# A DRAM-to-SBUF load that writes four copies of a triangular system to the partitions: one transfer, or one for each quarter

## The chip, the cores and the metric

The kernel runs on one core of one Trainium2 chip. The metric is device time in microseconds (us) of one execution, lower is better. The kernel before takes 2083.18 us, the median of three runs (2080.98 to 2087.81). The inputs lie in DRAM when the time starts, and the outputs must lie in DRAM when it ends.

## The reference

One layer of a hybrid encoder is applied to 2048 prompt frames and 32 sample frames of width 1024. The layer normalises its input, projects it to 6160 columns, runs two mixers on the result, attention over a band of nine 64-frame chunks (branch A) and a gated delta rule (branch B), and merges their outputs. The change touches branch B alone, and there the inverse of a unit lower triangular matrix for each head and each block of 64 frames:

```
m = jnp.einsum('nbhid,nbhjd->nbhij', k_beta, kb) * decay * strict
eye = jnp.eye(blk, dtype=f32)
t_inv = lax.linalg.triangular_solve(eye + m, jnp.broadcast_to(eye, m.shape),
                                    left_side=True, lower=True, unit_diagonal=True)
u = jnp.einsum('nbhij,nbhjd->nbhid', t_inv, v_beta)
```

The state of the rule then goes through the blocks in order, one step for each 64 frames.

## The kernel before

The prompt is done in two halves of 1024 frames; the sample frames ride with the second. Each half has a stage for branch B (`phase_b`) and one for branch A (`phase_a`). The large projections run beside both, so that TensorE (PE) always has matmuls to do: weights are loaded (`wraw`), scaled and split into two fp16 parts by ScalarE (ACT) and GpSimd (POOL), and multiplied into the PSUM banks `pj`. A last stage merges the branches and writes the output.

Python generators describe the pieces of work. A planner (`Flow`) runs them against a model of the engines and the transfers, and the order in which it emits instructions is the order of each engine's queue: every engine works through its queue in order and waits where an operand isn't there yet. All the transfers that this document speaks of are issued by SyncE's queue (SP in the profile, SPq for its issuing instructions), line 283, in `dma`. A transfer signals that it has landed on one of eight completion lanes, used in turn (`DMAHW0` to `DMAHW7`); an instruction that needs its data waits on that lane, and SP waits, before it gives a lane to a new transfer, until the lane's last transfer has landed.

In `phase_b` a block is one pair of heads and 512 frames, that is 16 triangular systems of 64 x 64. There are eight blocks in each half, and one more for the sample frames: 17 in all. For each block:

- `system` computes the matrices (`p_c`, on 128 partitions) and stores their diagonal 32 x 32 sub-blocks to DRAM, `sol_p`: 32 rows, one for each sub-block, of 1024 numbers each. Four transfers.
- `solve` clears `sys_u` on POOL, loads `sol_p` into `sys_p` four times over, to partitions 0 to 31, 32 to 63, 64 to 95 and 96 to 127 (lines 1236 and 1237), so that partition 32g + s holds system s and works on its columns g, g + 4, g + 8 and so on, and calls `substitute`.
- `substitute` is the forward substitution: 31 steps on VectorE (DVE) of a multiply into `sys_t` and a subtract from `sys_u`. The first instruction that reads `sys_p` is the 128 x 31 multiply `sys_t<-sys_p,sys_u`.
- The result goes to DRAM (`sol_u`), comes back in another shape (`tu`), and `inverse` builds the 64 x 64 inverses `u_bd` with it.
- `chain` runs the recurrence over the blocks. Each step is a ping-pong between PE and DVE: matmul into bank `x`, `r` on DVE, matmul with `u_bd`, `vn` on DVE, matmul, `state` on DVE. `tail` then normalises the outputs, loads the gate (`gb<-z`) and stores the product (`g<-gb`).

All of this shares DVE's queue with the convolutions (`acc`), the evacuations of projections (`zb`) and the weights' scales (`w_scale`).

Of the kernel before, what the change touches and what calls it, by code (L numbers as in the profile page):

```python
# [268 lines left out]
def trunk(ctx: ExitStack, tc: tile.TileContext, x_p, x_s, cache_k, cache_v, st_conv, st_gdn,  # L269
# [11 lines left out]
    def dma(dst, src, eng=nc.sync):  # L281

        eng.dma_start(dst, src)  # L283
        size = 2 if dst.dtype == F16 else 4
        n = size
        for k in dst.shape:
            n *= k

        n = max(n, n // (size * dst.shape[-1]) * 768)
        return flow.transfer("SP" if eng is nc.sync else "S", n)  # L290
# [495 lines left out]
    def phase_b(half):  # L786
# [438 lines left out]
        def solve():  # L1225
            while True:
                k, t = yield from q_sys.get()
                sys_p = bp.tile([P, 32, 32], F32, tag="sys_p", bufs=2, name="sys_p")
                sys_u = bp.tile([P, 8, 32], F32, tag="sys_u", bufs=2, name="sys_u")
                sys_t = bp.tile([P, 8, 32], F32, tag="sys_t", bufs=2, name="sys_t")  # L1230
                G.memset(sys_u[:], 0.0)
                for g in range(4):
                    G.memset(sys_u[g * 32:(g + 1) * 32].rearrange("p r i -> p (r i)")[:, g::36], 1.0)
                yield t
                p0 = pd[k.n % (2 * NP)][:]
                yield dma(sys_p[:].rearrange("p j i -> p (j i)"),
                          bass.AP(p0.tensor, p0.offset, [[0, 4], [1024, 32], [1, 1024]]))
                yield from substitute(sys_p, sys_u, sys_t)
                for g in range(4):
                    t = dma(ud[k.n % (2 * NP)][:].rearrange("s (r g i) -> g s r i", g=4, i=32)[g], sys_u[g * 32:(g + 1) * 32])  # L1240
                flow.start(inverse(k, t))

        def substitute(sys_p, sys_u, sys_t):
            for j in range(31):
                nr = j // 4 + 1
                w = 31 - j
                if nr == 1:
                    V.tensor_scalar(out=sys_t[:, 0, 0:w], in0=sys_p[:, j, j + 1:32], scalar1=sys_u[:, 0, j:j + 1],
                                    scalar2=None, op0=ALU.mult)
                else:  # L1250
                    V.tensor_tensor(out=sys_t[:, 0:nr, 0:w], in0=sys_u[:, 0:nr, j:j + 1].to_broadcast([P, nr, w]),
                                    in1=sys_p[:, j:j + 1, j + 1:32].to_broadcast([P, nr, w]), op=ALU.mult)
                yield
                V.tensor_tensor(out=sys_u[:, 0:nr, j + 1:32], in0=sys_u[:, 0:nr, j + 1:32],
                                in1=sys_t[:, 0:nr, 0:w], op=ALU.subtract)
                yield
# [179 lines left out]
        for g in (worker(todo), worker(decays), prep(), local(), solve(), solve()):  # L1436
            flow.start(g)
# [878 lines left out]
```

## Time and profile before

| | before |
|---|---|
| median of three runs | 2083.18 us |
| the profiled execution's own time | 2081.13 us |
| its span, first to last instruction | 2079.4 us |
| PE busy | 1969.9 us (95%) |
| DVE busy | 1456.5 us (70%) |
| ACT busy | 977.0 us (47%) |
| POOL busy | 709.3 us (34%) |
| mean granted clock of PE | 0.982 |
| DMA engines' mean share | 31.7% (the queue of SP's transfers) |
| loads `sys_p<-sol_p` | 17 of 512.0 KB, issued from 141.3 to 1247.5 us |

Times inside the execution count from its first instruction. An engine's waits are told as idle time before an instruction, with the one that released it in brackets. A stretch row gives busy time and count of instructions of each engine, the clock granted to PE (1.00 is full), the mean busy share of the core's 16 DMA engines and the bytes moved per second.

### The profile page before, as it was taken

The numbers are of one execution on the slowest core, as the hardware profiler recorded it, in microseconds if no ns is written. First come the engines' busy times: TensorE is split into PE (matmuls) and PEld (weight loads), VectorE is DVE, ScalarE is ACT, GpSimd is POOL, SyncE is SP. The second block draws the span as 40 slices with busy tenths as digits, with TensorE's granted clock in tenths as the row PEclk, the third lists the DMA queues.
The fourth block names the chain that finished last, engine by engine and source line by source line (L and its number), as shares of the span: only waits on it lengthen the run. The fifth ranks groups of instructions, "written<-read, shape, count | busy, mean of one in ns | idle before, by whom it ended". The sixth has DMA issues, their size and how long they took to land. (4 is left out here: it accounts for less than half of the span.)

```text
span 2079.4 us, 41810 instructions
## 1 busy us (share of the span) xinstructions
PE 1969.9 (95%) x15098; PEld 1419.4 (68%) x15098; DVE 1456.5 (70%) x4673; ACT 977.0 (47%) x2098; POOL 709.3 (34%) x1075
## 2 busy tenths in 40 slices
PE   4899999999999999899999899999999999999998
PEld 3455666667465666566677676767667678999996
DVE  7579888874267667768998887347657677655565
ACT  5565645444466668564544434346566642111110
POOL 5254443423322123334333323311110224644443
PEclk9899999999999999999999999999999999999999
DMA  3132332232323333222233233332332345433331
GB/s 109 62 98 80 98 107 65 82 82 87 121 68 122 92 87 101 66 72 73 78 85 88 73 91 95 97 91 76 87 89 82 108 139 196 135 105 113 111 123 48
DMA packets 197724, 196.53 MB, mean 95 GB/s; under 512 B 79623, under 2 KB 147571, under 8 KB 197517
## 3 DMA queue, kind: packets, MB, share of 16 engines
q1 hardware_dynamic: 197516, 193.85, 31.7%
q8 instruction: 119, 1.95, 0.4%
q14 instruction: 89, 0.72, 0.1%
HBM read 135.91 MB, written 50.53 MB: 90 GB/s over the span
## 5 line engine op out<-in xcount | busy, mean ns | idle before, releaser
L260 PE MATMUL pj<-hi,whi 128*128 128x512 f16 (+2 forms) x1992 | 654.3, 344 | 12.6 <-POOL whi L260 2.4
L260 PE MATMUL pj<-hi,wlo 128*128 128x512 f16 (+2 forms) x1952 | 644.4, 342 | 2.0 <-POOL wlo L260 1.9
L260 PEld LDWEIGHTS <-whi 128*128 128x128 f16 x3984 | 412.7, 105 | 222.2 <-issue 11.1
L260 PE MATMUL pj<-lo,whi 128*128 128x512 f16 (+2 forms) x1992 | 461.3, 339 | 0.0
L260 POOL TENSOR_TENSOR wlo<-wraw,whi 128x256 f16<-128x256 f32 x384 | 263.8, 708 | 570.9 <-ACT whi L260 328.4
L260 PEld LDWEIGHTS <-wlo 128*128 128x128 f16 x1952 | 207.1, 106 | 112.6 <-issue 11.2
L260 ACT CAST mh<-sg 128x256 fp32r<-128x256 f32 x64 | 26.0, 407 | 273.7 <-DVE sg L260 273.7
L260 ACT ACTIVATE wraw<-wraw,w_scale 128x1024 f32<-128x1024 f32 (+1 forms) x98 | 111.5, 1138 | 64.9 <-DVE w_scale L260 51.9
L260 ACT CAST ph<-b 128x512 f16<-128x512 f32 (+2 forms) x224 | 92.9, 422 | 100.2 <-PE b L260 95.4
L260 PE MATMUL a<-ghi,whi 128*128 128x256 f32 (+1 forms) x512 | 132.5, 290 | 4.9 <-DVE sg L260 4.7
L260 DVE TENSOR_TENSOR pl<-b,ph 128x512 f16<-128x512 f32 (+2 forms) x224 | 107.2, 485 | 37.9 <-ACT ph L260 36.8
L260 PE MATMUL a<-ghi,wlo 128*128 128x256 f32 (+1 forms) x512 | 130.6, 286 | 1.1 <-DVE wlo L260 1.1
L260 ACT CAST whi<-wraw 128x512 f16<-128x512 f32 (+1 forms) x196 | 119.6, 611 | 23.4 <-PE pj L260 20.5
L260 DVE TENSOR_TENSOR sys_u<-sys_u,sys_t 128x60 f32<-128x60 f32 (+24 forms) x527 | 123.3, 240 | 6.1
L260 POOL TENSOR_TENSOR w_scale<-w_scale,mhalf 128x1 f32<-128x1 f32 x49 | 32.4, 662 | 257.0 <-DVE w_scale L260 204.0
L260 ACT ACTIVATE sb<-sb,mx,unit 128x640 f32<-128x640 f32 (+4 forms) x128 | 108.8, 851 | 20.7 <-DVE mx L260 20.3
L260 DVE SCALAR_TENSOR_TENSOR acc<-raw,cwT,acc 128x512 f32<-128x512 f32 x144 | 112.0, 777 | 5.2 <-ACT acc L260 4.1
L260 DVE TENSOR_TENSOR sys_t<-sys_u,sys_p 128x60 f32<-128x60 f32 (+20 forms) x459 | 111.2, 246 | 5.9
L260 PEld LDWEIGHTS a<-ghi,whi 128*128 128x128 f32 x512 | 98.2, 192 | 7.3 <-DVE sg L260 7.0
L260 ACT COPY v_t<-o 128x64 f32<-128x64 f32 x132 | 27.6, 209 | 157.0 <-PE o L260 113.1
L260 PE MATMUL b<-ident,sb 128*128 128x128 f32 x560 | 99.3, 277 | 1.9 <-DVE ga L260 0.9
L260 PEld LDWEIGHTS a<-ghi,wlo 128*128 128x128 f32 x512 | 97.8, 191 | 1.9 <-DVE wlo L260 1.6
(350 smaller groups left out, 4237.0 us busy)
## 6 DMA issues: line engine op xcount, KB each, us to landing
wraw<-in_w_in SPq DMA_DIRECT2D x192, 256.0 KB
sg<-sig SPq DMA_DIRECT2D x112, 128.0 KB
sig<-sig SPq DMA_DIRECT2D x44, 256.0 KB
sys_p<-sol_p SPq DMA_DIRECT2D x17, 512.0 KB
x<-in_x_p SPq DMA_DIRECT2D x16, 512.0 KB
xt<-in_x_p SPq DMA_DIRECT2D x16, 512.0 KB
out_y_p<-xt SPq DMA_DIRECT2D x16, 512.0 KB
glo<-g SPq DMA_DIRECT2D x14, 512.0 KB
```

Source lines behind the costliest of these rows:

```text
L260: r = f(*a, **k)
```

## The change

The one transfer to 128 partitions, whose source pattern names the 32 rows four times (`[0, 4]`, `[1024, 32]`, `[1, 1024]`), becomes four transfers of the same 32 rows, each to one quarter of the partitions. The bytes written, 512 KB for a block, stay the same.

```
                 yield t
                 p0 = pd[k.n % (2 * NP)][:]
-                yield dma(sys_p[:].rearrange("p j i -> p (j i)"),
-                          bass.AP(p0.tensor, p0.offset, [[0, 4], [1024, 32], [1, 1024]]))
+
+                for g in range(4):
+                    t = dma(sys_p[g * 32:(g + 1) * 32].rearrange("p j i -> p (j i)"),
+                            bass.AP(p0.tensor, p0.offset, [[1024, 32], [1, 1024]]))
+                yield t
                 yield from substitute(sys_p, sys_u, sys_t)
```

The planner's order comes out the same: PE, DVE, ACT and POOL have the same instructions in the same order in both kernels, and SP has the same transfers in the same order, with three more at each of the 17 places. What moves is the lane that a transfer gets, and with it the names of the lanes that are waited for.

SP's queue at the eighth block (first half; `z` and `gb` belong to the tail and the gate, `wraw` to the next weights), before and then changed:

```order
L283 DMA z_87<-zb 128x512 [waits DVE_49]
L283 DMA sys_p<-sol_p_621 128x1x1024 [waits DMAHW6_49,DMAHW7_49,DMAHW5_49,DMAHW0_49]
L283 DMA wraw<-in_w_in 128x512 [waits DMAHW3_49,Activation_49,Pool_49]
L283 DMA wraw<-in_w_in 128x512 [waits DMAHW4_49]
L283 DMA gb<-z_86 64x2x256 x2
L283 DMA z_87<-zb 128x512 [waits DVE_49]
```

```order
L283 DMA z_87<-zb 128x512 [waits DVE_49]
L283 DMA sys_p<-sol_p_621 32x1024 [waits DMAHW4_49,DMAHW5_49,DMAHW3_49,DMAHW2_49]
L283 DMA sys_p<-sol_p_621 32x1024 [waits DMAHW0_49]
L283 DMA sys_p<-sol_p_621 32x1024 [waits DMAHW1_49]
L283 DMA sys_p<-sol_p_621 32x1024
L283 DMA wraw<-in_w_in 128x512 [waits Activation_49,Pool_49]
L283 DMA wraw<-in_w_in 128x512
L283 DMA gb<-z_86 64x2x256
L283 DMA gb<-z_86 64x2x256 [waits DMAHW6_49]
L283 DMA z_87<-zb 128x512 [waits DMAHW7_49,DVE_49]
```

The first quarter still waits for the four stores of `sol_p`; behind the quarters come the same transfers as before.

SP's queue at the seventh block of the second half, before and then changed:

```order
L283 DMA gcb<-gc_dram 64x512 [waits DMAHW5_49]
L283 DMA sys_p<-sol_p_10523 128x1x1024 [waits DMAHW6_49,DMAHW7_49,DMAHW1_49,DMAHW0_49]
L283 DMA gb<-z_85 64x2x256 x2
L283 DMA z_86<-zb 128x240 [waits DVE_49]
L283 DMA wraw<-in_w_in 128x512 [waits DMAHW2_49,Activation_49,Pool_49]
```

```order
L283 DMA gcb<-gc_dram 64x512 [waits DMAHW7_49]
L283 DMA sys_p<-sol_p_10547 32x1024 [waits DMAHW2_49,DMAHW3_49,DMAHW1_49,DMAHW0_49]
L283 DMA sys_p<-sol_p_10547 32x1024 x3
L283 DMA gb<-z_85 64x2x256 [waits DMAHW4_49]
L283 DMA gb<-z_85 64x2x256 [waits DMAHW5_49]
L283 DMA z_86<-zb 128x240 [waits DMAHW6_49,DVE_49]
L283 DMA wraw<-in_w_in 128x512 [waits DMAHW7_49,Activation_49,Pool_49]
```

The loads `gb<-z` now stand four transfers behind the first load of `sys_p` instead of one, and wait for lanes by name.

DVE's queue at that block, before and then changed (`state` is a step of the recurrence, which waits for PE):

```order
L260 SCALAR_TENSOR_TENSOR v_s<-e,acc 128x32 [waits Activation_49]
L260 TENSOR_SCALAR sys_t<-sys_p,sys_u 128x31 [waits DMAHW6_49]
L260 SCALAR_TENSOR_TENSOR state<-state,sc,x 128x64 [waits PE_49]
L260 TENSOR_TENSOR sys_u<-sys_u,sys_t 128x8x3 [waits DVE_49]
L260 TENSOR_TENSOR sys_u<-sys_u,sys_t 128x31 [waits DMAHW1_49,DMAHW7_49,DMAHW0_49,DVE_49]
```

```order
L260 SCALAR_TENSOR_TENSOR v_s<-e,acc 128x32 [waits Activation_49]
L260 TENSOR_SCALAR sys_t<-sys_p,sys_u 128x31 [waits DMAHW2_49,DMAHW3_49,DMAHW1_49,DMAHW0_49]
L260 SCALAR_TENSOR_TENSOR state<-state,sc,x 128x64 [waits PE_49]
L260 TENSOR_TENSOR sys_u<-sys_u,sys_t 128x8x3 [waits DVE_49]
L260 TENSOR_TENSOR sys_u<-sys_u,sys_t 128x31 [waits DVE_49]
```

The instructions stand where they stood; the first multiply waits for four lanes instead of one.

## The prediction

> **What bounds the kernel now.** I read the page first, then the waits, then three stretches of the queues.
>
> ```profile
> PE 1969.9 (95%) x15098; PEld 1419.4 (68%) x15098; DVE 1456.5 (70%) x4673; ACT 977.0 (47%) x2098; POOL 709.3 (34%) x1075
> sys_p<-sol_p SPq DMA_DIRECT2D x17, 512.0 KB
> ```
>
> PE sets the time: it is idle for 2079.4 - 1969.9 = 109.5 us in all, so a change off PE can only give back a part of that, plus what PE loses when its clock is lowered. The list of waits says what the 17 loads cost directly:
>
> ```profile
> DVE sys_t L260 <- DMA sys_p<-sol_p: 9.4, 3, 4.8
> ACT sig L260 <- DMA z<-zb: 4.8, 1, 4.8
> ```
>
> So 14 of the 17 loads land before DVE asks for them and are worth nothing there; three are late, by 9.4 us together. The second row matters because of where it lies, as the third place shows. The load itself, first block, in SP's queue and by stretches (columns: stretch, busy us and count for PE, PEld, DVE, ACT and POOL, PE's clock, DMA share, GB/s):
>
> ```profile
> 141.26 0.63 SPq L283 DMA_DIRECT2D sys_p<-sol_p  x1
> 152.53 0.81 SPq L283 DMA_DIRECT2D wraw<-in_w_in  x2
> ...
> 141.00:143.00 2.00, 2.00 (x14) 1.13 (x13) 1.52 (x5) 1.42 (x3) 0.13 (x1) 1.00 0.93 340
> 147.00:149.00 2.00, 2.00 (x11) 0.90 (x10) 1.83 (x6) 1.72 (x4) 1.94 (x5) 1.00 0.25 102
> 149.00:152.00 3.00, 3.00 (x15) 1.35 (x14) 3.00 (x7) 1.54 (x4) 2.03 (x3) 1.00 0.01 5
> ```
>
> Nothing was issued between 141.26 and 152.53, so what moves from 147 to 149 us is this load: a share of 0.25, 4 engines of 16, at 102 GB/s, while other transfers just before it reached 0.93 and 340 GB/s. Its 524,288 bytes need 5.1 us at the one rate and 1.5 us at the other. It keeps four engines busy while twelve are idle, and whatever is issued behind it also needs those four.
>
> The three late places. The last number of a DVE or PE row is the idle time before it.
>
> ```profile
> 424.99 0.56 SPq L283 DMA_DIRECT2D sys_p<-sol_p  x1
> 437.48 0.24 DVE L260 TENSOR_SCALAR sys_t<-sys_p,sys_u 128x31 f32<-128x31 f32 x1 [4.25 <-DMA sys_p<-sol_p]
> 437.72 0.28 DVE L260 SCALAR_TENSOR_TENSOR r<-x,negc,v_t 128x64 f32<-128x64 f32 x1
> 438.06 0.44 PE L260 MATMUL x<-r,u_bd 128*128 128x64 f32 x2 [3.43 <-DVE r L260]
> ...
> 1183.53 0.56 SPq L283 DMA_DIRECT2D sys_p<-sol_p  x1
> 1195.00 0.24 DVE L260 TENSOR_SCALAR sys_t<-sys_p,sys_u 128x31 f32<-128x31 f32 x1 [4.83 <-DMA sys_p<-sol_p]
> 1195.16 0.27 DVE L260 SCALAR_TENSOR_TENSOR state<-state,sc,x 128x64 f32<-128x64 f32 x1
> 1195.48 0.69 PE L260 MATMUL x<-state,k_bd 128*128 128x64 f32 x2 [4.48 <-DVE state L260]
> ...
> 975.33 0.56 SPq L283 DMA_DIRECT2D sys_p<-sol_p  x1
> 975.94 8.33 SPq L283 DMA_DIRECT2D z<-zb  x2
> 987.30 0.48 DVE L260 TENSOR_SCALAR sys_t<-sys_p,sys_u 128x31 f32<-128x31 f32 x1 [0.37 <-DMA sys_p<-sol_p]
> 987.63 0.69 ACT L260 ACTIVATE sig<-pj,w_half 128x512 f32<-128x512 f32 x1 [4.80 <-DMA z<-zb]
> 988.37 0.28 PE L260 MATMUL pj<-hi,whi 128*128 128x272 f16 x1 [0.90 <-ACT sig L260]
> ```
>
> Call them A (425), B (1183) and C (975). From issue to use the load takes 437.48 - 424.99 = 12.49, 1195.00 - 1183.53 = 11.47 and 987.30 - 975.33 = 11.97 us. At A and B the recurrence stands behind the late multiply in DVE's queue (`r`, `state`), and PE stands behind the recurrence with all its projections. At C a store of `z` issued 0.61 us behind the load lands just when the load does, and holds a buffer that ACT, and then PE, needs.
>
> PE's idle time isn't the whole price:
>
> ```profile
> 438.00:442.00 4.00, 3.94 (x18) 3.44 (x19) 2.39 (x17) 0.96 (x1) 0.56 (x1) 0.57 0.22 79
> 442.00:446.00 4.00, 3.82 (x23) 2.17 (x21) 3.12 (x14) 1.90 (x6) 2.30 (x4) 1.00 0.21 33
> 1195.50:1199.60 4.10, 4.10 (x19) 3.14 (x20) 2.43 (x15) 1.38 (x3) 0.00 (x0) 0.51 0.35 110
> 1199.60:1204.00 4.40, 4.40 (x47) 3.78 (x46) 2.83 (x15) 1.94 (x4) 0.00 (x0) 1.00 0.46 98
> ```
>
> After each of the two long stalls PE works for some 4 us at about half its clock, busy for 3.94 of 4.00 and 4.10 of 4.10 us, so this is lost too.
>
> **The change, part by part.** *What a load costs then.* No row of before shows a 32-row load to a quarter, so I bound it.
>
> ```profile
> 1.52 1.77 SPq L283 DMA_DIRECT2D x<-in_x_p  x4
> 5.28 0.69 DVE L260 BATCH_NORM_STATS2 st<-x 128x6 f32<-128x512 f32 x1 [0.46 <-DMA x<-in_x_p]
> 1703.74 2.60 DMA sg<-sig
> 1726.88 6.68 DMA xt<-in_x_p
> 441.05 2.54 SPq L283 DMA_DIRECT2D sol_u<-sys_u  x4
> sg<-sig SPq DMA_DIRECT2D x112, 128.0 KB
> xt<-in_x_p SPq DMA_DIRECT2D x16, 512.0 KB
> ```
>
> Four loads of rows of 4 KB are issued in 1.77 us, 0.44 each; four issues of many small pieces take 2.54 us, 0.64 each. So the last quarter goes out 1.3 to 1.9 us after the first. From there a load of a quarter's size, 128 KB, takes 2.60 us in the chain of waits (`sg`). A load of all 512 KB, the first `x`, was used 3.76 us after its issue (5.28 - 1.52), with three like it behind it; the longest in the chain took 6.68 (`xt`). The last quarter is there at 1.3 + 2.6 = 3.9 us at best and 1.9 + 6.68 = 8.6 at worst after the first issue. I take 5: the quarters are like `sg` in size and like `x` in company.
>
> *What that removes.* DVE is ready for the load 12.49 - 4.25 = 8.24 us after its issue at A, 11.47 - 4.83 = 6.64 at B, 11.97 - 0.37 = 11.60 at C. At 5 us all three waits go. At 8.6 us A keeps 0.4 and B 2.0 us. The lowered clock goes with the stalls.
>
> - A: 3.43 idle + 4.00 x (1 - 0.57) = 1.72, together 5.15 us.
> - B: 4.48 + 4.10 x (1 - 0.51) = 2.01, together 6.49 us.
> - C: 0.90 us; the store of `z` goes out about 1.3 us later, behind the quarters, and finds all the engines soon free.
>
> The Trainium skill, page TensorE: Matmul & The Clock Gate, section Part 1: The HAM clock gate, says that the clock is halved after an idle window of about 3.4 us that runs freely, whatever the kernel does. By that, a gap of 3.43 us as at A meets a whole window only by chance, and the sum would be 1.72 us smaller in executions where it doesn't; the profiled one has the halved clock at both places, and the sum goes by it.
>
> *What it adds.* 51 issues on SP, 51 x 0.44 = 22 us over the execution. SP has room for them (nothing goes out from 141.9 to 152.5), and only what stands directly behind a load is later, by 1.3 us; it lands earlier all the same, since it no longer sits behind 5 us of transfer on four engines. DVE's first multiply waits for four lanes, three waits more:
>
> ```profile
> L260 DVEq EVENT_SEMAPHORE  x3: 21/50/50, 437.5 to 437.7; - x3
> ```
>
> 51 x 0.05 = 2.6 us at most on DVE, mostly while it would wait anyway, and DVE is idle for 30% of the span. I put it at nothing; if it all fell on the path it would be 2.6 us.
>
> *What is late next.* PE's work after A and B must be able to start earlier. These are the stretches behind them:
>
> ```profile
> 442.00:540.00 98.00, 97.17 (x705) 63.54 (x704) 45.95 (x192) 41.80 (x88) 34.02 (x51) 1.00 0.32 93
> 540.00:860.00 320.00, 310.62 (x2412) 192.43 (x2411) 219.85 (x770) 203.03 (x429) 84.10 (x126) 0.99 0.31 92
> 1199.60:1290.00 90.40, 87.57 (x783) 66.58 (x782) 76.64 (x324) 36.20 (x86) 29.55 (x50) 1.00 0.34 90
> 1290.00:1600.00 310.00, 304.72 (x2755) 217.31 (x2754) 177.32 (x617) 169.91 (x397) 53.44 (x82) 1.00 0.29 83
> ```
>
> PE is busy for 97 to 99% there, so it, and no other engine, sets the pace, and DVE moves up with it. After B DVE is at 85% (76.64 of 90.40); if anything takes some of B back, it is DVE. Nothing in this kernel starts at a fixed time, so an earlier PE stays earlier.
>
> Sum: 5.15 + 6.49 + 0.90 = 12.5 us, from the profiled execution's own 2081.13 (span 2079.4) to 2068.6. That execution lies 2.05 us under the median of the three runs, 2083.18; against the median the forecast is 2070.6. With the bounds (A and B keep 2.4 us, the 2.6 us of lane waits) the loss is at most 5 us: 2075.6. On the other side nothing reaches beyond the sum but the spread of the runs.
>
> **The rivals.** *The gain is half.* The next wait takes what the load gives back: DVE after B, or a shorter gap of PE that still lowers its clock. For it speaks DVE at 85%, against it that PE has no gap in the rows after either place. Worth B or A alone, about 6 us: 2077.
>
> *The quarters queue behind one another.* If four transfers follow each other with the full 2.60 us each, the last one lands 4 x 2.60 = 10.4 us after the first issue; A keeps 10.4 - 8.24 = 2.2 and B 10.4 - 6.64 = 3.8 of their waits. Gain about 3 us: 2080, no change that can be told. Against it: the four `x` loads above went out in 1.77 us, and the first was there in 3.76. The Trainium skill, page DMA: Bandwidth & Descriptors, section Rules for kernel authors, speaks for this rival: two transfers to disjoint halves of the partitions serialize on the same 16 engines, and one transfer to 128 partitions is better. The same section says that an outermost dimension of size c below 16, such as a broadcast of c copies, keeps a transfer on c engines at most; the share of 0.25 agrees with that, and then the one transfer is not the 16-engine transfer that the first rule has in mind.
>
> *Slower: the quarters get no more engines.* If a quarter, too, runs on 4 of the 16 engines, and all on the same four, the bytes take the same 5.1 us and everything is 3 x 0.44 = 1.3 us later: three stalls grow by 1.3, and so do the stores and loads behind. Worth 3 x 1.3 = 4 us and more clock: 2087 or more. It decides from the point where the last quarter lands more than 11.5 us after the first issue. Against it: the source's outermost dimension of four copies is gone, and the rows' share of 0.93 comes from loads without it.
>
> **How the numbers follow.** A change under 0.3%, 6.2 us, can't be told from none here. Chances: the forecast 0.74 (2065 to 2076), half the gain 0.13, queueing quarters 0.08, no more engines 0.05. The range takes in the spread of the runs below the sum, 2064.5, and half the gain above, 2078. Faster by over 0.3% (under 2076.9): nearly all of the forecast and half of the half gain, 0.80; within 0.3%: the other half, the queueing quarters and a part of the rest, 0.16; slower 0.04.
>
> **What would show it.** Right: the first multiply of `sys_t` follows the last issue of `sys_p` by less than 7 us where DVE waits for it, or DVE has no such wait left; stretches after an issue have a DMA share far over 0.25; PE's gaps at A and B are gone and its clock is 1.00 behind them; SP has 68 issues of `sys_p` of 128 KB. Wrong: `sys_t<-sys_p` still stalls by more than 2 us at B; or both stalls are gone and PE has new gaps of like size within the next 100 us; or transfers behind `sys_p` land later than now.

## The result and the profile after

| | before | after |
|---|---|---|
| median of the runs compared | 2084.25 us | 2071.72 us |
| lowest and highest | 2080.98 to 2088.89 | 2068.95 to 2076.6 |
| the profiled execution's own time | 2081.13 us | 2071.35 us |
| its span | 2079.4 us | 2069.6 us |
| PE busy | 1969.9 us | 1969.5 us |
| span less PE's busy time | 109.5 us | 100.1 us |

The ratio of after to before is 0.9941, with a 95% interval of 0.9922 to 0.996: the changed kernel is faster by 8 to 16 us. The two medians differ by 12.53 us.

From the page of after (engines; DMA issues with their median from issue to landing), and from its view of the tile `sys_p` (shortest, median and longest time of a quarter from issue to landing):

```profile
PE 1969.5 (95%) x15098; PEld 1420.1 (69%) x15098; DVE 1458.4 (70%) x4673; ACT 978.4 (47%) x2098; POOL 710.7 (34%) x1075
sys_p<-sol_p SPq DMA_DIRECT2D x68, 128.0 KB, 3.2
DMA to landing us min/median/max: 2.5/3.2/5.1
```

The list of waits has no row for `sys_p<-sol_p` any more, nor the one of ACT's `sig` for `z<-zb`. What it has for loads of the same part of the program are two short ones that before did not have:

```profile
ACT whi L260 <- DMA gb<-z: 1.8, 1, 1.8
DVE gb L260 <- DMA gb<-z: 1.3, 1, 1.3
```

The first block in SP's queue, and the stretches behind it (columns as in the prediction: stretch, busy us and count for PE, PEld, DVE, ACT and POOL, PE's clock, DMA share, GB/s):

```profile
140.43 1.82 SPq L283 DMA_DIRECT2D sys_p<-sol_p  x4
151.71 0.83 SPq L283 DMA_DIRECT2D wraw<-in_w_in  x2
...
143.00:144.00 1.00, 1.00 (x6) 0.45 (x6) 0.83 (x5) 0.33 (x1) 0.61 (x2) 1.00 0.77 254
144.00:145.50 1.50, 1.50 (x8) 0.73 (x7) 0.24 (x2) 1.44 (x2) 1.50 (x3) 1.00 0.20 49
145.50:147.50 2.00, 2.00 (x13) 1.11 (x11) 1.21 (x3) 1.46 (x3) 1.89 (x5) 1.00 0.00 0
```

Before, the load still moved at a share of 0.25 between 147 and 149 us, 5.7 to 7.7 us after its issue. Now the share is 0.77 about 3 us after the first issue, and 5 us after it nothing moves. By the completion events of the trace the whole load, counted from the first of its four issues to the landing of the last quarter, takes 4.07 to 7.12 us over the 17 blocks; the one transfer took 8.7 to 12.5.

Place A: SP, then DVE, then PE (time, duration, engine; an idle time before the row would stand at its end).

```profile
424.18 1.73 SPq L283 DMA_DIRECT2D sys_p<-sol_p  x4
432.34 0.43 DVE L260 TENSOR_SCALAR sys_t<-sys_p,sys_u 128x31 f32<-128x31 f32 x1
432.78 0.27 DVE L260 SCALAR_TENSOR_TENSOR r<-x,negc,v_t 128x64 f32<-128x64 f32 x1
433.21 0.60 PE L260 MATMUL b<-ident,v_t 128*128 128x128 f32 x4
433.65 0.33 PE L260 MATMUL x<-r,u_bd 128*128 128x64 f32 x2
...
437.60 0.43 PE L260 MATMUL o<-state,q_bd 128*128 128x64 f32 x2 [0.82 <-ACT v_t L260]
433.60:437.60 4.00, 3.18 (x24) 2.31 (x23) 2.90 (x21) 1.88 (x3) 0.65 (x2) 1.00 0.26 80
```

Place B in the same way, with the row of PE that follows the recurrence's next step:

```profile
1177.21 1.87 SPq L283 DMA_DIRECT2D sys_p<-sol_p  x4
1184.21 0.39 DVE L260 TENSOR_SCALAR sys_t<-sys_p,sys_u 128x31 f32<-128x31 f32 x1
1184.56 0.28 DVE L260 SCALAR_TENSOR_TENSOR state<-state,sc,x 128x64 f32<-128x64 f32 x1
1184.74 0.38 PE L260 MATMUL pj<-lo,whi 128*128 128x512 f16 x1
1184.95 0.37 PE L260 MATMUL x<-state,k_bd 128*128 128x64 f32 x2
...
1184.60:1188.70 4.10, 4.10 (x37) 3.40 (x36) 3.75 (x23) 2.87 (x7) 0.00 (x0) 1.00 0.43 138
```

No idle time stands at the ends of the multiplies or of the matmuls behind them. The multiply comes 432.34 - 424.18 = 8.16 us after the first issue at A and 7.00 us at B, which is when DVE gets to it; by the completion events the last quarter had landed 3.1 us earlier at A and 2.1 us earlier at B. The clock behind is 1.00 at both, where it was 0.57 and 0.51. One small gap is new, 0.82 us 4 us behind A.

Place C: SP, DVE, ACT and PE.

```profile
970.66 1.85 SPq L283 DMA_DIRECT2D sys_p<-sol_p  x4
972.62 0.37 SPq L283 DMA_DIRECT2D z<-zb  x1
983.01 0.23 DVE L260 TENSOR_SCALAR sys_t<-sys_p,sys_u 128x31 f32<-128x31 f32 x1
980.46 0.69 ACT L260 ACTIVATE sig<-pj,w_half 128x512 f32<-128x512 f32 x1 [2.78 <-PE pj L260]
983.47 0.28 PE L260 MATMUL pj<-hi,whi 128*128 128x272 f16 x1
```

The store of `z` goes out 1.96 us behind the first quarter instead of 0.61 us behind the load. By the completion events it lands 6.9 us after the load's first issue instead of 12.2. ACT's idle time before the same `sig` now ends with a matmul and not with the store, and PE has no idle time before its own row. The same holds for what stands directly behind the load at B: the first `gb<-z` lands 5.3 us after the load's first issue instead of 11.7.

**Where the 9.8 us of the two profiles lie.** PE does the same matmuls in the same order, so the same matmul's start in the two traces, subtracted, says how far after is ahead at that point. Rows of before, then of after:

```profile
545.33 0.63 PE L260 MATMUL b<-ident,vs 128*128 128x128 f32 x4 [2.82 <-DVE vs L260]
973.70 0.28 PE L260 MATMUL pj<-hi,whi 128*128 128x272 f16 x1 [1.94 <-DVE zb L260]
1190.63 0.38 PE L260 MATMUL pj<-lo,whi 128*128 128x512 f16 x1
1201.56 0.33 PE L260 MATMUL x<-r,u_bd 128*128 128x64 f32 x2
1627.11 0.28 PE L260 MATMUL b<-ident,kr 128*32 128x128 f32 x1 [0.84 <-ACT ro L260]
```

```profile
539.91 1.08 PE L260 MATMUL b<-ident,vs 128*128 128x128 f32 x4 [2.82 <-DVE vs L260]
969.07 0.28 PE L260 MATMUL pj<-hi,whi 128*128 128x272 f16 x1 [1.95 <-DVE zb L260]
1189.09 0.33 PE L260 MATMUL x<-r,u_bd 128*128 128x64 f32 x2
1614.51 0.28 PE L260 MATMUL b<-ident,kr 128*32 128x128 f32 x1 [0.84 <-ACT ro L260]
```

| stretch (time in before) | ahead at its end | gained in it | what lies in it |
|---|---|---|---|
| to 545.33 | 5.42 | +5.42 | A |
| to 973.70 | 4.63 | -0.79 | no late load; PE's clock |
| to 1190.63 (1184.74 in after) | 5.89 | +1.26 | C; PE's clock at two places |
| to 1201.56 | 12.47 | +6.58 | B |
| to 1627.11 | 12.60 | +0.13 | no late load |
| to the end of the span | 9.8 | -2.8 | no late load; PE's clock; the end behind the last matmul |

What was gained at A and B is what those places lost before. The losses lie elsewhere, most of them behind gaps that are as long in after as in before (2.82, 1.94 and 0.84 us in the rows above). They come from PE's clock behind these gaps; rows of before, then of after, each a stretch of 4 us from the end of such a gap:

```profile
545.40:549.40 4.00, 4.00 (x24) 2.36 (x25) 1.75 (x6) 0.91 (x2) 0.72 (x1) 1.00 0.40 133
973.70:977.70 4.00, 4.00 (x32) 3.18 (x32) 3.86 (x16) 1.48 (x3) 0.00 (x0) 1.00 0.92 223
1627.10:1631.10 4.00, 3.99 (x33) 3.26 (x34) 1.75 (x8) 2.84 (x7) 1.15 (x1) 1.00 0.64 226
```

```profile
540.00:544.00 4.00, 4.00 (x15) 2.14 (x16) 0.69 (x1) 0.59 (x1) 0.00 (x0) 0.59 0.38 131
969.20:973.20 4.00, 4.00 (x23) 3.07 (x22) 3.89 (x15) 1.63 (x3) 0.00 (x0) 0.59 1.05 224
1614.60:1618.60 4.00, 4.00 (x21) 2.73 (x22) 1.07 (x5) 2.04 (x4) 1.26 (x2) 0.57 0.61 220
```

PE is busy in all six, at full clock in before and at 0.57 to 0.59 in after: 4.00 x 0.41 = 1.64 us twice and 4.00 x 0.43 = 1.72 us, 5.0 us lost. At two other places it is before that has the lowered clock (0.58 at 848 to 852 us, 0.64 at 1096 to 1100 us) and after has 1.00: 1.68 + 1.44 = 3.1 us gained; and after has 0.74 at 821.3 to 825.3 us, 1.0 us lost. On balance the clock at these places takes 2.9 us from this pair of profiles, and 9.8 + 2.9 = 12.7 us. This count is not complete. It leaves out two losses of after, 1.2 us behind 1389.8 us (clock 0.50 up to 1393.2 us, 1.00 in before) and 1.0 us between the last matmul and the end, and two gains that no load explains, 0.8 us from before A and 1.3 us at a gap ahead of 1542.76 us that is 1.48 us in before and 0.21 us in after. Place by place, the starts of the same matmuls give 4.6 us at A, 6.6 at B and about 1.6 around C, 12.8 us together. Whether the clock's part is an effect of the change or differs from execution to execution is the question of the last experiment.

### The profile page after: what moved, and what is told of

It is laid out like the page before. It is cut to its first block, busy times and chain, and to the rows that moved or that the text cites. A ratio compares the mean times of both kernels' runs of the same rounds, so it can differ in the third digit from the quotient of the medians.

```text
span 2069.6 us, 41878 instructions
## 1 busy us (share of the span) xinstructions
PE 1969.5 (95%) x15098; PEld 1420.1 (69%) x15098; DVE 1458.4 (70%) x4673; ACT 978.4 (47%) x2098; POOL 710.7 (34%) x1075
## 3 DMA queue, kind: packets, MB, share of 16 engines
q8 instruction: 119, 1.95, 0.4%
```

## The experiments

All of them keep the program's order and change only how `sys_p` is loaded. Ratios are to the kernel before, run on the same chip in the same batch; the first batch (the changed kernel again, its two halves, the columns in order) has 2088.63 us for it, the second (rows outermost, columns reversed, two pairs, eighths) 2082.88 us. The difference between batches is one more reason to compare ratios only.

| kernel | median us | ratio | 95% interval | profiled span | DVE's waits for the load |
|---|---|---|---|---|---|
| the change, again | 2075.07 | 0.9942 | 0.9921 to 0.9962 | 2073.3 | none |
| quarters only at A and B | 2072.31 | 0.993 | 0.9907 to 0.9954 | 2074.8 | none |
| quarters everywhere but A and B | 2088.45 | 0.9998 | 0.9983 to 1.0014 | 2080.3 | 7.5 us, 2 times |
| four by columns | 2077.02 | 0.9952 | 0.9935 to 0.9969 | 2076.2 | none |
| four by columns, last first | 2081.27 | 0.9993 | 0.9979 to 1.0007 | 2080.0 | 6.2 us, 2 times |
| one, rows outermost | 2074.87 | 0.9962 | 0.9947 to 0.9978 | 2073.1 | none |
| two pairs | 2132.57 | 1.0238 | 1.0202 to 1.0275 | 2128.3 | 49.4 us, 13 times |
| eight of 16 rows | 2071.93 | 0.9951 | 0.9937 to 0.9965 | 2071.3 | none |

### The two places alone, and all the others alone

The theory is that the gain lies at A and B, the eighth block of the first half and the seventh of the second. The rival is that it is spread over the 17 loads, through DMA engines that come free earlier. One kernel has the quarters at A and B only, the other everywhere else; the first in outline as a diff against the change, the second has `not in`:

```
-                for g in range(4):
-                    t = dma(sys_p[g * 32:(g + 1) * 32] ...
+                if (half, k.n) in ((0, 7), (1, 6)):
+                    for g in range(4): ...          # the four quarters
+                else: ...                           # the one transfer of before
```

> Quarters at A (first half, eighth block) and B (second half, seventh block) alone; the other 15 loads stay one transfer. Theory (the gain is the two stalls on PE's path and their slow clock, 5.15 + 6.49 us): the stalls at A and B are gone, the one at C stays (DVE 0.4 us, ACT about 4.8 us), and the time is 8 to 12 us under the kernel before, ratio 0.994 to 0.996. Rival (the gain is spread over all 17 loads, because the transfers behind them no longer queue on four engines): 2 of 17 parts, at most 2 us, ratio 0.999 or more.

> Quarters everywhere but at A and B. Theory: both stalls are there as before, 4.2 and 4.8 us of DVE, with PE's gaps of 3.4 and 4.5 us; only C is gone. Time within 2 us of the kernel before, ratio 0.999 to 1.001. Rival (spread over all loads): 15 of 17 parts, about 10 us less, ratio 0.995.

With the quarters at A and B alone the ratio is 0.993, all of the change's gain; I had expected 0.994 to 0.996. At C ACT still waits for `z`, but 3.6 us instead of the 4.8 expected, and DVE has no wait for the load there. With 15 of 17 loads in quarters and these two as before it is 0.9998, none of it. The two stalls are there again, that at B shorter than before (2.99 against 4.83 us); DVE's rows in that kernel:

```profile
438.59 0.24 DVE L260 TENSOR_SCALAR sys_t<-sys_p,sys_u 128x31 f32<-128x31 f32 x1 [4.49 <-DMA sys_p<-sol_p]
1198.06 0.24 DVE L260 TENSOR_SCALAR sys_t<-sys_p,sys_u 128x31 f32<-128x31 f32 x1 [2.99 <-DMA sys_p<-sol_p]
```

The gain is at A and B; the spread-out gain falls. The other 45 issues cost nothing that shows: 0.9998 holds them all, and takes in at most 0.0014 x 2088.6 = 2.9 us of loss.

### Four transfers that stay on four engines

To tell the number of transfers from the number of engines, four transfers of a quarter of the columns each, whose source still has the four copies outermost:

```
+                for c in range(0, 1024, 256):
+                    nc.sync.dma_start(flat[:, c:c + 256],
+                        bass.AP(p0.tensor, p0.offset + c, [[0, 4], [1024, 32], [1, 256]]))
```

> Four transfers for each load as in the change, but each to all 128 partitions and to a quarter of the columns, so that each still names the four copies in its outermost dimension; the same issues, the same lanes, pieces of 1 KB instead of 4. Theory (the copies in the outermost dimension hold a transfer to 4 engines): DMA share 0.25 again, the first multiply at A and B waits 1.3 us longer than before or more (5.5 and 6.1 us), time 3 to 8 us over the kernel before, ratio 1.001 to 1.004. Rival (several smaller transfers in flight are what helps): as the change, stalls gone, ratio 0.994.

My expectation was wrong: 0.9952, and no stall at the multiply. The load as a whole is no faster, 8.8 to 10.1 us from the first issue to the last landing, against 8.7 to 12.5 for the one transfer. But the first multiply belongs to the first of 31 steps, whose numbers lie in the first columns, and so it waits for the first of the four transfers alone. At A it starts at 432.1 us, and the last columns land 1.7 us later; at B 2.5 us later. I had counted the wait as one for the whole load. A smaller stall is left behind B: DVE is idle for 1.73 us until 1192.42 us, when the `gb<-z` issued behind the four pieces lands, and PE stops for 1.42 us; with the quarters both are absent.

So the same kernel with the last columns first (`for c in (768, 512, 256, 0)`), which makes the multiply wait for everything again:

> The four transfers by columns, with the last columns issued first, so that the columns that the first multiply reads land last. Theory after the run by columns in their order (four engines all the same, 9.1 to 10.1 us for all; the gain came from the first part being there early): the multiply now waits for all four, 9.1 to 10.1 us after the first issue and 1.3 to 2 us later than the one transfer counted from the last issue; stalls of 2 to 6 us stay at A and B, ratio 0.998 to 1.003. Rival (four transfers on four queues are quicker in themselves, whatever their engines): the stalls are gone, ratio under 0.997.

The waits, and a stretch in which only the load moves:

```profile
DVE sys_t L260 <- DMA sys_p<-sol_p: 6.2, 2, 3.6
...
147.00:149.00 2.00, 2.00 (x11) 0.94 (x10) 1.94 (x6) 2.00 (x5) 1.31 (x3) 1.00 0.27 94
```

0.9993: the stalls are back, 2.68 us at A and 3.57 at B, and the gain is gone as far as the interval tells (at most 0.0021 x 2082.9 = 4.4 us of it left). The share of 0.27 is that of the one transfer (0.25). This is what the prediction's rival "the quarters get no more engines" describes. Its price of 2087 us was too high: the four pieces on four engines land no later than the one (8.6 to 10.9 us), so the stalls did not grow by 1.3 us. Of the two columns kernels together: four issues by themselves bring nothing; what counts is when the part that the first multiply reads is there.

### The leading dimension of the source

What is left is why a quarter is quick. If the number of copies at the front of the source pattern sets the number of engines, one transfer with the rows first must be quick, and two transfers with two copies each must be slow. As one transfer, and as two:

```
+                nc.sync.dma_start(flat, bass.AP(p0.tensor, p0.offset,
+                                  [[1024, 32], [0, 4], [1, 1024]]))
```

```
+                for g in range(2):
+                    nc.sync.dma_start(flat[g * 64:(g + 1) * 64],
+                        bass.AP(p0.tensor, p0.offset, [[0, 2], [1024, 32], [1, 1024]]))
```

> One transfer for each block, as before, but its source names the 32 rows first and the four copies second, so that partition 4s + g gets system s. The systems then stand on other partitions than the rest of the program takes them to, so the outputs are not the reference's; instructions, bytes and order are those of the kernel before. Theory (a leading dimension of four keeps the transfer on four engines, and that is what makes it late): the load runs on all the engines, lands 2.5 to 7 us after its issue instead of 8.7 to 12.5, DVE has no wait over 1 us for it, and the time is that of the four quarters or a little below, ratio 0.992 to 0.996. Rival (it is the number of transfers, or that the first multiply waits for pieces that land one by one): one transfer stays late, 8 us or more, the two stalls of 4.3 and 4.8 us stay, ratio 0.998 to 1.001.

> Two transfers, each of two copies to 64 partitions, leading dimension of the source 2. Theory (a leading dimension of c keeps a transfer on c engines): a transfer runs on two engines, the DMA share alone is 0.12 to 0.25 depending on whether the two transfers get the same two engines or different ones; on the same two the load lands 13 to 18 us after the issue, A and B stall by 8 to 11 us and others of the 17 loads are late too, ratio 1.004 to 1.02; on two different pairs it is as before, ratio 0.999 to 1.002. Rival (cutting the load into pieces helps of itself): between before and the quarters, ratio 0.995 to 0.998.

The first block in the one, with the stretch in which its end moves; then the waits and stretches of the other:

```profile
141.33 0.60 SPq L1237 DMA_DIRECT2D sys_p<-sol_p  x1
...
144.00:145.00 1.00, 1.00 (x6) 0.44 (x5) 0.85 (x6) 0.43 (x1) 0.63 (x1) 1.00 0.83 332
```

```profile
DVE sys_t L260 <- DMA sys_p<-sol_p: 49.4, 13, 8.9
ACT sig L260 <- DMA z<-zb: 9.0, 1, 9.0
...
148.00:150.00 2.00, 2.00 (x11) 0.93 (x10) 1.94 (x5) 1.97 (x5) 1.45 (x3) 1.00 0.13 49
150.00:152.00 2.00, 2.00 (x11) 0.88 (x9) 2.00 (x5) 1.01 (x2) 1.52 (x2) 1.00 0.13 51
```

One transfer of the same 512 KB with the rows first moves at a share of 0.83 and 332 GB/s and lands 3.5 to 6.2 us after its issue; before has a share of 0.37 in the same stretch, so little else moves there. Two transfers of two copies move at 0.13 of the engines, 2 of 16, both of them together: 50 GB/s, half of the one transfer's 102. They land 13.7 to 17.1 us after the first issue; 13 of 17 loads are late, by 49.4 us together. The kernel takes 1.0238, 49.7 us more: PE's idle time rises from 109.5 to 2128.3 - 1986.9 = 141.4 us, and its busy time by 17.0 us at a lower clock. That is more than I had expected (1.004 to 1.02), since I had thought of A, B and a few others and not of 13 blocks.

So it is the leading dimension: four copies in front, a share of 0.25; two in front, 0.13; 32 rows in front, 0.83. The completion events say the same: a transfer of this load leaves 5 of them with four copies in front, 3 with two, and 16 with rows in front, one transfer or four or eight. Cutting the load is a way to have the rows in front, and not the cause; cut the other way it is a loss of 50 us. The rows-first kernel comes out at 0.9962 with no stall, just over what I expected (0.992 to 0.996); its interval overlaps that of the quarters, and why its middle lies higher is not settled.

### Eight transfers

```
+                for g in range(8):
+                    nc.sync.dma_start(flat[g * 16:(g + 1) * 16],
+                        bass.AP(p0.tensor, p0.offset + g % 2 * 16 * 1024, [[1024, 16], [1, 1024]]))
```

> Eight transfers of 16 rows, 64 KB each, to 16 partitions each; 119 issues more than before instead of 51. Theory (issues cost 0.44 us each on SP, which has room, and the last issue sets the landing): issues spread over 3.1 us, all landed 5.5 to 8 us after the first issue, no wait at A (slack there 8.2 us), at most 1 us at B (6.6 us), ratio 0.993 to 0.998, the same as the quarters or up to 2 us more. Rival (more transfers cost by the lanes they take from others): new waits for gb, z or wraw on DVE or ACT, ratio 0.999 or more.

0.9951, as the quarters. The whole load lands 5.3 to 7.9 us after the first issue; the last issue goes out 3.1 to 4.9 us after the first; at B it is there 1.8 us before DVE wants it, so the room is nearly used up. 119 issues more than before, and eight lanes taken at a time, cost nothing that can be told.

### Does the clock behind the other gaps belong to the change?

Three more profiles, without an edit: the changed kernel twice (the first with times), the kernel before once.

> The changed kernel once more, for a second profile. Theory: DVE has no wait for sys_p, PE's clock is 1.00 behind A and B, ratio about 0.994. In the first profile of the changed kernel PE's clock was 0.58 to 0.71 behind four gaps that the change does not touch (541 to 545, 824 to 828, 970 to 974, 1614 to 1618 us), where the kernel before had 1.00. If the halved clock depends on where a gap falls in a window that runs freely, at least one of the four has 1.00 this time. Rival: the program itself sets it, and the same four have the same clocks within 0.1.

> The kernel before, a second profile. Question: whether PE's clock behind the gaps that the change doesn't touch is set by the program or differs from execution to execution. In the first profile of before it was 1.00 behind the gaps near 545, 827, 974 and 1617 us and lowered behind the one near 850 us. Theory (it differs from execution to execution): at least two of these five are in the other state now, while the two stalls of 4 to 5 us at 425 to 438 and 1184 to 1195 us are there as before. Rival (the program sets it): all five as in the first profile, so that the lowered clock in the changed kernel is an effect of the change.

> The changed kernel, a third profile, for the same question. Theory: of the places near 541, 824, 846, 972 and 1616 us at least one is in another state than in the first profile of the changed kernel (lowered, lowered, 1.00, lowered, lowered). No wait of DVE for the load in any case, and the load landed 4 to 7.2 us after its first issue.

PE's clock in the 4 us from the end of each of the five gaps, which have the same length in all five profiles:

| gap (its length) | before | before, 2nd | after | after, 2nd | after, 3rd |
|---|---|---|---|---|---|
| near 545 us (2.82) | 1.00 | 0.58 | 0.59 | 0.60 | 0.60 |
| near 825 us (0.81) | 1.00 | 1.00 | 0.74 | 0.72 | 0.72 |
| near 848 us (1.41) | 0.58 | 0.57 | 1.00 | 1.00 | 1.00 |
| near 974 us (1.95) | 1.00 | 0.58 | 0.59 | 0.59 | 0.58 |
| near 1627 us (0.84) | 1.00 | 1.00 | 0.57 | 1.00 | 0.57 |
| own time of the execution | 2081.13 | 2091.09 | 2071.35 | 2075.03 | 2071.8 |

The second profile of before, the stretch behind the first gap, and one further up that begins 4 us behind a gap of 0.74 us:

```profile
551.80:555.80 4.00, 3.87 (x14) 1.91 (x15) 0.69 (x1) 0.58 (x1) 0.00 (x0) 0.58 0.38 131
288.00:292.00 4.00, 4.00 (x25) 3.65 (x25) 1.63 (x7) 0.00 (x0) 1.95 (x3) 0.50 0.00 0
```

For the gaps near 545 and 974 us, and near 1627, the clock differs between executions of one kernel, so it isn't the change that set it: the first profile of before happened to have full clock at both of the former. It also had it at 288 to 292 us, where the second profile of before and the second of after have 0.50 and 0.52. For the pair near 825 and 848 us the clock went with the kernel in all five profiles, lowered behind one of the two and full or nearly full behind the other; the exchange is worth 1.68 - 1.04 = 0.6 us in favour of after. It doesn't hang on the two stalls, though: the kernel with eight transfers, which has neither, shows 1.00 and 0.62 there, as before does, and 1.00 behind the gap near 545 us. The third profile of after was to differ from the first somewhere; it does not at these five places.

The traces show more of this than the stretches of 4 us do. In each of the twelve traces all changes of PE's clock, as its events record them, lie on a grid of 3.41 us, to 0.001 us, and where the grid lies differs from trace to trace. In the first and the third profile of after it lies within 0.1 us, counted from the span's start, and these are the two whose five clocks agree. Two windows of that grid at the gap of 2.82 us, in after and then in before:

```profile
536.47:539.88 3.41, 0.62 (x3) 0.10 (x1) 2.03 (x4) 2.24 (x4) 1.30 (x2) 1.00 0.21 79
539.88:543.29 3.41, 3.38 (x10) 1.73 (x11) 0.69 (x1) 0.59 (x1) 0.00 (x0) 0.50 0.45 154
```

```profile
540.77:544.18 3.41, 1.74 (x9) 0.59 (x6) 1.13 (x1) 1.85 (x3) 0.71 (x2) 1.00 0.09 34
544.18:547.59 3.41, 2.26 (x14) 1.43 (x15) 1.59 (x5) 0.98 (x3) 0.72 (x2) 1.00 0.56 192
```

In after the gap lies in one window, in which PE is busy for 0.62 us, and the next window has the clock at 0.50. In before the same gap is split over two windows with 1.74 and 2.26 us of work, and the clock stays. So how a gap falls on the grid counts beside its length. PE's busy time in the window doesn't settle every case: 1.47 us was followed by 1.00 near 974 us in before, 1.46 us by 0.50 at the same gap in after.

## Why the prediction was right

It forecast 2070.6 us against the median and the runs gave 2071.72. By its steps:

- **What bounds the kernel: right.** PE's busy time is the same (1969.9 and 1969.5 us) and its idle time fell by 9.4 us. The two kernels with the quarters at A and B alone, and everywhere else, show that 15 of the 17 loads are worth nothing that the times can tell.
- **The load's time: 5 us taken, 3.9 to 8.6 as bounds; measured 4.07 to 7.12.** It was above 5 in 12 of the 17 blocks: 5.07 at A, 4.89 at B and 6.57 at C. At B that left 2.1 us to spare before DVE got to it. The issues are 1.3 to 1.5 us apart, first to last, as assumed (1.3 to 1.9), but 2.1 to 2.65 us at four of the 17, where SP's issues were held up between them. None of these is A, B or C.
- **A, 5.15 us: measured 5.42 up to 545 us**, and some 0.8 of that was there before A, in the rows of PE just ahead of the two stalls (434.02 in before, 433.21 in after, the matmul into `b`). So 4.6 us net: the stall and its clock are gone, and 0.82 us of new gap at 437.60 gives part back. **B, 6.49 us: measured 6.58.** **C, 0.90 us: gone**, but no steady part of the gain: the second profile of before has DVE waits for the load at A and B alone, ACT's wait for `z` there is 2.4 us instead of 4.8, and PE does not stop. In the first profile a second gap of PE stood just ahead, 0.68 us at 984.07 behind DVE's `z_s`; it is gone in after too, so that C and its surroundings gave 1.6 us.
- **The lowered clock as part of the price: right.** In the second profile of before PE stood 3.77 us at A and 3.53 at B, with a clock of 0.50 and 0.61 behind; with the columns reversed 1.87 and 3.22 us were followed by 0.72 and 0.67. Where the stall at B was 2.64 us (quarters everywhere but A and B), the clock behind it was 1.00. So it is not a fixed sum for each stall.
- **51 issues and three more lane waits at nothing: right within the interval**, by the kernel with quarters everywhere but A and B and by the eighths. The only new waits of this kind in after are the two for `gb<-z`, 3.1 us together; PE has no gap of half a microsecond or more at either place (269 and 521 us). That the transfer behind a load would land earlier in spite of its later issue was right too: `z` at C after 6.9 us instead of 12.2, `gb` at B after 5.3 instead of 11.7.
- **Nothing takes the gain back later: right for the program, missed for the clock.** From B to 1627 us after even gained 0.13 us. I had taken PE's clock in the rest of the program as the same in both executions. It isn't: 2.9 us went the other way in this pair of profiles at the places counted above, which is most of why the spans differ by 9.8 us and not by the sum of 12.5, while the medians, over several executions, differ by 12.53. That this meets 12.5 to a tenth is luck: the interval of the ratio runs from 8 to 16 us.

The rivals. *Half the gain*: no stall that took the other's place was found, and DVE, the one named, was at 91% in the first 4.10 us behind B (3.75) while PE was busy for all of them. *The quarters queue*: the last quarter landed at 4.07 to 7.12 us and not 10.4. The Trainium skill, page DMA: Bandwidth & Descriptors, section Rules for kernel authors, speaks for it: two transfers to halves of the partitions serialize, and one to 128 partitions is better. Here four transfers beat one, so the rule as it stands would have kept the slower kernel; the same section's other rule, that an outermost dimension of c copies keeps a transfer on at most c engines, is the one that decides, and it agrees with all three measured shares (0.25 for four, 0.13 for two, 0.83 for 32 rows). *No more engines*: the reversed columns show what it would have given, no change, rather than 2087.

On the clock, the Trainium skill, page TensorE: Matmul & The Clock Gate, section Part 1: The HAM clock gate, says that the windows run freely, so that one kernel shows different phases from run to run. The trace agrees as far as the clock behind one and the same gap differed between executions of one kernel. It also names one idle window of about 3.4 us as the condition for the lowered clock; here gaps of 0.84 to 2.82 us had it behind them, so the length of the gap alone doesn't tell. The grid of 3.41 us in the traces, not at one and the same place in all of them, agrees with windows that run freely, but a window needn't be idle from end to end: in the rows above one with 0.62 us of work was enough.

## What to carry to other kernels

A transfer that repeated its source by a pattern with the copies outermost ran on as many DMA engines as there were copies, here four and two. Put the rows outermost, by one transfer for each copy or by the order of the pattern, and look for a DMA share as low as copies/16 in a stretch where nothing else moves. Before pricing such a change, look which of the transfers are waited for at all (3 of 17 here), and what the first waiting instruction reads: it may be enough that its part lands first. When two single profiles are subtracted, take out the stretches where PE is busy with nothing changed but its clock, or use medians of several executions.

## What I had not expected of the hardware

- Two transfers of two copies each ran on the same two engines, at a share of 0.13 with both outstanding, and not on two each.
- PE's clock was lowered behind gaps as short as 0.84 us, and stayed at 1.00 behind one of 2.82 us in another execution. The means of 0.57 to 0.60 over 4 us are a clock of 0.50 for one window of 3.41 us; where PE is busy all through it, it costs about 1.7 us, as much as a fair-sized gap.
- Executions of the kernel before, with the same order of work, lay between 2074.1 and 2094.6 us over the batches. Of its two profiled ones, the slower is already 3.8 us behind the other at 385 us, before the first late load, and 3.2 us of lag arose in the stretch from 286 to 293 us, where its clock was lowered (0.52 from 286 to 292 us) and the other's was 1.00.
